# A pooling mixer's output projection: P7 of six blocks as seven smaller products that share P1's and P6's time

## The chip, the cores and the metric

The kernel runs on one core of a Trainium2 chip. The metric is the device time of one execution in microseconds (us). A core has a matrix engine (TensorE, PE in the profile; its weight loads have a row of their own, PEld), three engines for elementwise work (VectorE or DVE, ScalarE or ACT, GpSimd or POOL) and SyncE (SP), which here issues most of the DMAs. Each engine works through its own list of instructions in order; an instruction that waits holds up everything behind it on that engine.

## The reference

One layer of a streaming encoder over x, 4096 rows of 1024 columns, all in float32:

```python
normed = rms_norm(x, norm_w)
u, gate = split(normed @ in_w, 2)               # in_w: 1024 x 2048
pooled = trailing means of u over 2, 4, 8, 16 rows (by column group) - u
mixed = einsum('bsgc,gcd->bsgd', pooled, group_w) + group_b
y = mixed * scale * silu(gate)
out = rms_norm(x + y @ out_w, final_norm_w)     # out_w: 1024 x 1024
```

What this case is about is the last line: the product `y @ out_w`, the addition of x and the closing norm. The kernel calls it the output stage.

## The kernel before, in words

**Seven products.** Each large product is computed as a Winograd form of Strassen's scheme: both operands are cut into quarters, and seven products P1 to P7 of quarter-sized operands (sums and differences of the quarters) take the place of eight. A product's operand is float32, split into a high and a low part (`split`: a copy on ScalarE, L175, then a subtraction on VectorE, L169), and multiplied in three passes, high by high, high by low, low by high (`mm3`, L779). Operand pairs lie in *op* tiles, a ring of four (`next_op`); the weights' pairs of all seven products stay in *w* tiles. Results collect in PSUM, in eight *banks* of 128 x 512. A sum of two products that the scheme wants is made in the bank itself: only P1 and P7 start their bank afresh, the others add to a bank that a copy has filled.

**Stages.** Two input stages, a and b (four blocks of 1024 rows each), make u and the gate, and pool and store y into the DRAM tiles *yd*. The output stage, o, has eight blocks of 512 rows, numbered 0 to 7, in the order P1, P7, P6, P2, P5, P4, P3 (`ORDER_OUT`). A whole product there is 24 matmuls with 512 columns: two row tiles of 128 rows, each with four inner steps of three passes. In `sets_of` a block gets four pairs of banks: x (P1, P2), v (P7, P4), y (P6, P5, P3, on top of a copy of P1's result) and a spare pair; the pairs rotate from block to block.

**What is done twice already.** A quarter-sized product can itself be cut into seven, with 42 matmuls of 256 columns in place of 24 of 512. The kernel before does that at one place of stage b (`product_seven`, L725, with a bank addition at L762), and for P2 of blocks 2 to 7 in the output stage (`product_inner`, L879). P2's five inner products P2, P3, P4, P1, P7 are issued in P2's place, P6 in the middle of P5 and P5 behind it; `add_inner` (L889) adds the latter two's banks to the row tiles on VectorE. `split_inner` makes the operands from one y tile: the plain quarters in one op tile, four sums in another. `load_inner` and `form_inner` make the inner weights in block 1, in four *st* tiles that are kept from then on (`kept`).

**Buffers.** Working tiles of 512 KB come from two first-in, first-out pools, `st` (11) and `vt` (8): `take()` gives the one longest free, `give()` returns one. Which data share a tile, and so who waits for whom, follows from the order of takes and gives in the program's text. A wait is on the last user of the tile: a load into a tile waits for the store that reads it.

**A block's data.** `load_o` takes four y tiles per block (quarters named 11, 21, 22, 12), each 512 KB, on SP's queue (L1045). The main loop runs it four products ahead (`load_reach`), and `split_o` two ahead (`split_reach`): while P1 of a block runs, P6's operand is being split, and so on, across blocks. For P7 `split_o` takes a further tile, subtracts (11 minus 21), and splits. `load_h` takes *row tiles*, two for each half of 256 rows, `hs[b][half, j]`; the result rows are collected in them. Before the last block only half 0 has a DMA there, of x's right half (256 KB each, L1056). x's other quarters are added by POOL's accumulating DMAs (`add_h`, L1062) after the eviction. The last block loads x outright (L1052).

**Eviction.** `evict_o` copies P7's, P6's and P2's banks to the row tiles (ScalarE), copies P1's to the pair y, and adds P5's, P4's and P3's banks to the row tiles (VectorE, L1245). After P4 (half 1) and P3 (half 0) `finish` ends the rows: two squares with their sums on ScalarE (L1121), each into a scratch tile from `take()`, a root (ScalarE L216, the rest on POOL, L217 to L235), two scalings on VectorE (L1125) and two stores on SP's queue (L1129). These run while the next block's P1 and P7 are on TensorE. The last block ends with finer pieces (`early_half` to `late_vector`, L1145 to L1204).

**Order.** A scheduler puts each engine's instructions in order, in the main by the order of the program's text and by dependences; `tc.issue_after(x)` adds the rule that what is inside comes after instruction x. `latest` is the last matmul, `latest_copy` and `latest_split` the last two halves of a split.

## Time and profile before

| | us |
|---|---|
| median of three timed runs | 909.32 |
| their range | 909.14 to 909.33 |
| the profiled execution's own time | 909.13 |
| span of the profiled execution | 907.3 |
| the difference, around the span | 1.8 |

The profile describes one execution. Its page gives each engine's busy time, then the span in 40 slices, the DMA queues, the chain of work that ended last, and the costliest groups of instructions: line, engine, operation, tiles (output <- inputs, without buffer numbers), shapes and count, then busy time, mean ns of one, and idle time before them with what ended it. "L779" is the line in the kernel's text, that of the helper where one is used. Matmuls overlap, so the mean of one is longer than the distance from one to the next. DMA groups give the time from issue to landing.

### The profile page before, as it was taken

The numbers are of one execution on the slowest core, as the hardware profiler recorded it, in microseconds if no ns is written. First come the engines' busy times: TensorE is split into PE (matmuls) and PEld (weight loads), VectorE is DVE, ScalarE is ACT, GpSimd is POOL, SyncE is SP. The second block draws the span as 40 slices with busy tenths as digits, with TensorE's granted clock in tenths as the row PEclk, the third lists the DMA queues.
The fourth block names the chain that finished last, engine by engine and source line by source line (L and its number), as shares of the span: only waits on it lengthen the run. The fifth ranks groups of instructions, "written<-read, shape, count | busy, mean of one in ns | idle before, by whom it ended". The sixth has DMA issues, their size and how long they took to land.

```text
span 907.3 us, 11824 instructions
## 1 busy us (share of the span) xinstructions
PE 898.9 (99%) x4392; PEld 790.2 (87%) x4392; DVE 731.5 (81%) x868; ACT 494.0 (54%) x760; POOL 83.9 (9%) x166
## 2 busy tenths in 40 slices
PE   9999999999999999999999999999999999999996
PEld 7888888888888888889889888888888898988986
DVE  3889896985995999798599499599759768868686
ACT  7869547447446565346545636545535435445434
POOL 0020100100110000000000000001122113112200
PEclk9999999999999999999999999999999999999998
DMA  9987667677575462323554475528585675775732
GB/s 341 401 303 238 251 229 229 215 270 251 224 267 198 161 217 85 110 100 116 206 189 148 176 267 168 192 70 232 173 232 172 171 192 158 169 220 162 175 140 92
DMA packets 71401, 179.41 MB, mean 198 GB/s; under 512 B 6576, under 2 KB 24624, under 8 KB 71344
## 3 DMA queue, kind: packets, MB, share of 16 engines
q1 hardware_dynamic: 58720, 146.13, 46.4%
q0 software_dynamic: 11904, 31.48, 13.5%
q10 hardware_dynamic: 720, 1.06, 0.3%
q8 instruction: 34, 0.56, 0.3%
q14 instruction: 23, 0.19, 0.1%
HBM read 117.81 MB, written 60.83 MB: 197 GB/s over the span
## 4 chain that ended last, share of the span: by engine, by line
PE 95%; DVE 2%; DMA 1%; ACT 1%; issue 0%; DVEq 0%; ACTq 0%
PE bank L779 89%; PE bank L879 3%; PE bank L725 2%; PE bank L421 1%; DMA st<-in_x 1%; DMA early<-in_wut 0%; ACT st L461 0%; DVE vt L1245 0%; ACT st L1152 0%; PE bank L487 0%; DVE vt L172 0%; DVE w L169 0%; ACT st L443 0%; ACT early L443 0%; DVE vt L1204 0%
## 5 line engine op out<-in xcount | busy, mean ns | idle before, releaser
L779 PE MATMUL bank<-op,w 128*128 128x512 f32 x2592 | 560.9, 379 | 0.0
L779 PEld LDWEIGHTS bank<-op,w 128*128 128x128 f32 x2592 | 489.4, 189 | 70.2 <-ACT vt L175 0.4
L779 PE MATMUL bank<-w,op 128*128 128x512 f32 (+1 forms) x1212 | 262.2, 377 | 0.0
L779 PEld LDWEIGHTS bank<-w,op 128*128 128x128 f32 x1212 | 226.0, 189 | 31.0
L169 DVE TENSOR_TENSOR op<-st,op 128x1024 fp32r<-128x1024 f32 x134 | 162.3, 1219 | 58.0 <-ACT op L175 57.6
L175 ACT ACTIVATE op<-st 128x1024 fp32r<-128x1024 f32 x134 | 140.2, 1052 | 113.4 <-PE bank L779 64.5
L175 ACT ACTIVATE vt<-bank 128x512 f32<-128x512 f32 (+1 forms) x115 | 65.8, 590 | 46.5 <-PE bank L779 43.1
L169 DVE TENSOR_TENSOR st<-st,st 128x1024 f32<-128x1024 f32 (+1 forms) x42 | 45.8, 1104 | 18.9 <-ACT st L256 16.8
L169 DVE TENSOR_TENSOR op<-vt,op 128x1024 fp32r<-128x1024 f32 x42 | 51.1, 1219 | 8.1 <-ACT op L175 8.1
L175 ACT ACTIVATE op<-vt 128x1024 fp32r<-128x1024 f32 x42 | 44.1, 1054 | 24.9 <-PE bank L779 20.9
L1062 POOL DMA_DIRECT2D st<-in_x x19 | 16.8, 893 | 387.0 <-DVE op L169 352.9
L175 ACT ACTIVATE st<-bank 128x512 f32<-128x512 f32 (+1 forms) x61 | 34.7, 585 | 30.6 <-PE bank L779 19.1
L175 ACT ACTIVATE bank<-bank 128x512 f32<-128x512 f32 (+1 forms) x60 | 32.1, 537 | 30.1 <-PE bank L779 26.0
L933 DVE TENSOR_TENSOR_SCAN vt<-vt,window 128x1040 f32<-128x1040 f32 x16 | 37.9, 2376 | 1.6 <-DMA yd<-vt 1.5
L169 DVE TENSOR_TENSOR w<-st,w 128x1024 fp32r<-128x1024 f32 (+1 forms) x26 | 30.8, 1198 | 9.2 <-ACT w L175 9.2
L175 ACT ACTIVATE w<-st 128x1024 fp32r<-128x1024 f32 (+1 forms) x26 | 26.6, 1035 | 17.4 <-PE bank L779 9.5
L175 ACT ACTIVATE vt<-tails 128x32 f32<-128x32 f32 x28 | 6.3, 228 | 46.8 <-DVE vt L933 25.7
L979 DVE SCALAR_TENSOR_TENSOR vt<-vt,vt 128x1024 f32<-128x1024 f32 x24 | 29.3, 1219 | 0.3
L172 DVE TENSOR_TENSOR st<-st,vt 128x1024 f32<-128x1024 f32 x22 | 26.1, 1215 | 3.4 <-DMA vt<-rd 3.4
L1125 DVE SCALAR_TENSOR_TENSOR vt<-vt,ors,st 128x1024 f32<-128x1024 f32 x18 | 22.5, 1282 | 7.6 <-POOL ors L235 7.6
L1245 DVE TENSOR_TENSOR st<-bank,st 128x512 f32<-128x512 f32 x23 | 15.8, 689 | 14.0 <-PE bank L779 14.0
L984 DVE SCALAR_TENSOR_TENSOR st<-vt,colt,st 128x512 f32<-128x512 f32 x38 | 26.8, 743 | 0.1
(143 smaller groups left out, 735.3 us busy)
## 6 DMA issues: line engine op xcount, KB each, us to landing
st<-in_xt SPq DMA_DIRECT2D x28, 512.0 KB, 6.3
sd<-st POOLq DMA_DIRECT2D x28, 512.0 KB, 4.0
st<-sd SPq DMA_DIRECT2D x26, 512.0 KB, 4.2
st<-in_x SPq DMA_DIRECT2D x20, 512.0 KB, 6.0
st<-yd SPq DMA_DIRECT2D x20, 512.0 KB, 4.6
yd<-st SPq DMA_DIRECT2D x19, 512.0 KB, 3.1
out<-vt SPq DMA_DIRECT2D x18, 512.0 KB, 4.6
st<-wod SPq DMA_DIRECT2D x15, 512.0 KB, 4.0
```

Source lines behind the costliest of these rows:

```text
L169: return nc.vector.tensor_tensor(out=dst, in0=a, in1=b, op=ALU.subtract)
L172: nc.vector.tensor_tensor(out=dst, in0=a, in1=b, op=ALU.mult)
L175: return nc.scalar.activation(dst, src, func)
L725: latest[0] = nc.tensor.matmul(cell(n, c).rearrange("p (a s) -> p a s", s=2), x1, x2, start=i == P1 and k + m == 0, stop=k == 1 and m == 2 ...
L779: latest[0] = nc.tensor.matmul(ps, a, b, start=start and n == 0, stop=stop and n == 2, skip_group_check=True).ins
L879: latest[0] = nc.tensor.matmul(ps, x1, x2, start=i in (P1, P7) and k + n == 0, stop=k == 1 and n == 2, skip_group_check=True,).ins
L933: nc.vector.tensor_tensor_scan(out=sums_[:, HIST:], data0=flat[:, HIST:], data1=flat[:, HIST - win : 2 * end - win], initial=first_sum, op ...
L979: nc.vector.scalar_tensor_tensor(out=s[:, :, at : at + H], in0=s[:, :, at : at + H], scalar=1.0 / win, in1=v[:, :, HIST:], op0=ALU.mult, o ...
L984: nc.vector.scalar_tensor_tensor(out=sg[:, j], in0=s[:, j, at : at + H], scalar=bias_c[2 * grp + j], in1=sg[:, j], op0=ALU.add, op1=ALU.mult,)
L1062: nc.gpsimd.dma_start(out=hs[b][half, j][:, n], in_=x[row_of(b, half, j), n * H : (n + 1) * H], accum_op=ALU.add,)
L1125: nc.vector.scalar_tensor_tensor(out=us[j], in0=us[j], scalar=rs[:, j : j + 1], in1=fw[0], op0=ALU.mult, op1=ALU.mult,)
L1245: partial["added"] = nc.vector.tensor_tensor(out=dst, in0=src, in1=dst, op=ALU.add).ins
```

## The change

- **P7 of blocks 2 to 7 becomes seven inner products**, which all collect in P7's own pair of banks, v. `split_own` makes the operands: four subtractions of 256 columns into a working tile, then two op tiles, plain quarters and sums, in place of one. `leaf` issues one inner product (6 matmuls of 256 columns) and is shared with P2's.
- **`own_first`**: inner P1 and P5 are issued inside P1, ahead of the last 6 of its 24 matmuls. Two moves on ScalarE follow: cell 1 to cell 0 in the banks (a cell is half a bank), and cell 3 to *m5*, a quarter of the first row tile of half 1, which P6 fills later (in block 7 a tile of its own).
- **`own_rest`**, in P7's place: inner P2 and P6, move of cell 1 to cell 2, `piece(0)` (the first 6 matmuls of P6), inner P7 and P3, move of cell 2 to cell 3, `piece(1)` (6 more of P6), inner P4, and on VectorE an addition of m5 to both halves of bank 1 of the pair. P6 then has 12 matmuls left.
- **Inner weights**: P7's are formed in block 1 as well, ahead of P2's (`forming`): their raw tiles are loaded, summed in place, and split into three kept tiles and a quarter of P7's own w tiles. P2's follow, the last of them in block 2's P1. Six kept st tiles take the place of four.
- **P2's inner products**: their order becomes P2, P4, P1, P3, P7, and their sums are split later (`late_split`, called when the main loop is at P6), the plain quarters where they were.
- **Row tiles**: before the last block, `load_h` runs at P1 (half 1) and P2 (half 0) of the block itself, in `run`, in place of four products ahead in `load_o`.

The diff, without the inner weights' formation and the rewriting of P2's operand tables:

```diff
+    def split_own(u):
+        at = u.rearrange("p (g k) (j c) -> p g j k c", g=2, j=2)
+        b11, b12, b21, b22 = (at[:, g, j] for g in range(2) for j in range(2))
+        v = take("p (n k c) -> p n k c", n=4, k=2)
+        sub(v[:, 0], b12, b11)
+        sub(v[:, 1], b22, v[:, 0])
+        sub(v[:, 2], b22, b12)
+        sub(v[:, 3], b21, v[:, 1])
+        plain_op = next_op("p (s g k j c) -> p s g j k c", s=2, g=2, k=2, j=2)
+        split(plain_op.rearrange("p s g j k c -> p s (g k) (j c)"), u)
+        sums_op = next_op("p (s n k c) -> p s n k c", s=2, n=4, k=2)
+        split(sums_op, v)
...
+    def own_into(i, n, start=False):
+        leaf(own["t"], own_w, i, own["v"][n % 2], n // 2, start)
...
+    def own_move(dst, src):
+        with tc.issue_after(own.get("moved", latest_copy[0])):
+            own["moved"] = copy(own["m5"] if dst is None else own_cell(dst), own_cell(src)).ins
+
+    def own_first(t, b, sets):
...
+        own_into(P1, 1, True)
+        own_into(P5, 3)
+        if b == NBO - 1:
+            own["held"] = take()
+            own["m5"] = own["held"][:, 0, 0:256]
+        else:
+            own["m5"] = hs[b][1, 0][:, 0, 0:256]
+        own_move(0, 1)
+        own_move(None, 3)
+
+    def own_rest(piece):
+        own_into(P2, 0)
+        own_into(P6, 1)
+        own_move(2, 1)
+        piece(0)
+        own_into(P7, 2)
+        own_into(P3, 1)
+        own_move(3, 2)
+        piece(1)
+        own_into(P4, 2)
+        bank = own["v"][1].rearrange("p (j b) -> p j b", j=2)
+        add(bank, bank, own["m5"].unsqueeze(1).to_broadcast([P, 2, 256]))
...
-            for p in (P2, P3, P4, P1, P7):
+            for p in (P2, P4, P1, P3, P7):
                 product_inner(p)
...
         elif i == P2:
             s["12"] = load_y(b, 0, 1)
-            load_h(b, 1)
-        elif i == P5:
+            if b == NBO - 1:
+                load_h(b, 1)
+        elif i == P5 and b == NBO - 1:
             load_h(b, 0)
...
+            if b > 1:
+                t = split_own(s["3"])
+                give(s.pop("3"))
+                return t
...
-        if kind == "o":
+        if kind == "o" and b < NBO - 1 and i in (P1, P2):
+            load_h(b, int(i == P1))
+        if kind == "o" and b > 1 and i == P1:
+            t = split_up.pop(n)
+            out_part(P1, t, sets["x"][0], 0, range(4))
+            out_part(P1, t, sets["x"][1], 1, range(2))
+            own_first(split_up.pop(n + 1), b, sets)
+            with tc.issue_after(latest[0]):
+                out_part(P1, t, sets["x"][1], 1, range(2, 4))
+            evict_o(b, i, sets)
+        elif kind == "o" and b > 1 and i == P7:
+            def piece(m):
+                with tc.issue_after(latest[0]):
+                    out_part(P6, split_up[n + 1], sets["y"][0], 0, range(2 * m, 2 * m + 2))
+            own_rest(piece)
+            evict_o(b, i, sets)
...
+            while b > 0 and len(gathered) < 6 and st.free and len(st.free) + len(vt.free) > 4:
+                gathered.append(st.keep())
+                kept.append(gathered[-1])
...
+        if kind == "o" and i == P6 and late_split:
+            late_split.pop()()
```

More of the change, by code (lines that the diff above doesn't have):

```diff
@@ new lines, with leaf @@
+    own = {}
+    def leaf(t, ws, i, bank, half, start=False):
+        ps = bank.rearrange("p (a s) -> p a s", s=2)[:, half * P : (half + 1) * P]
+        with tc.issue_after(latest[0]):
+            for k in range(2):
+                a = [o[:, k] for o in t[i]]
+                b = [o[:, k].rearrange("p s a -> p a s") for o in ws[i]]
+                for n, (x1, x2) in enumerate(((a[0], b[0]), (a[0], b[1]), (a[1], b[0]))):
+                    latest[0] = nc.tensor.matmul(
+                        ps, x1, x2, start=start and k + n == 0, stop=k == 1 and n == 2,
+                        skip_group_check=True,
+                    ).ins
@@ L867, in product_inner @@
+    def own_rest(piece):
[10 more added lines that the diff above has]
+        add(bank, bank, own["m5"].unsqueeze(1).to_broadcast([P, 2, 256]))
+        if "held" in own:
+            give(own.pop("held"))
     def product_inner(i):
-        t, sets = inner["t"], inner["sets"]
+        sets = inner["sets"]
@@ L892, in sets_bank, with out_part @@
         return inner["sets"]["spare"][n]
+    def out_part(i, t, dst, j, ks, cols=slice(0, H // 2), apart=False):
+        rows = slice(j * P, (j + 1) * P)
+        for k in ks:
+            wk = w[i][k // 2]
+            mm3(
+                dst,
+                (t[:, 0, k, rows], t[:, 1, k, rows]),
+                (wk[:, 0, k % 2], wk[:, 1, k % 2]),
+                (i in (P1, P7) or apart) and k == 0,
+                k == 3,
+                cols,
+            )
     def product_out(i, t, sets, last):
```

159 lines of the change are left out of this document (89 added, 70 removed).

## Prediction

> **What bounds the kernel now.** I read the page first, then TensorE's timeline over the output stage, then busy time block by block. In a timeline row stand the start, the length, the engine, the line, the operation, its tiles and how many were merged, and in brackets the idle time before it and what ended it; in a row of stretches its length, then the busy time of PE, PEld, DVE, ACT and POOL.
>
> ```profile
> PE 898.9 (99%) x4392; PEld 790.2 (87%) x4392; DVE 731.5 (81%) x868; ACT 494.0 (54%) x760; POOL 83.9 (9%) x166
> PEclk9999999999999999999999999999999999999998
> PE 95%; DVE 2%; DMA 1%; ACT 1%; issue 0%; DVEq 0%; ACTq 0%
> ...
> 701.02 1.50 PE L879 MATMUL bank<-w,op 128*128 128x256 f32 x12
> 702.36 0.83 PE L879 MATMUL bank<-inner,op 128*128 128x256 f32 x6
> ...
> 710.89 26.07 PE L779 MATMUL bank<-w,op 128*128 128x512 f32 x120
> 736.79 1.50 PE L879 MATMUL bank<-w,op 128*128 128x256 f32 x12
> ...
> 701.02:736.79 35.77, 35.77 (x188) 31.91 (x186) 26.13 (x34) 17.61 (x27) 7.22 (x16) 1.00 0.80 216
> 736.79:772.56 35.77, 35.77 (x188) 31.91 (x186) 27.35 (x35) 17.53 (x27) 9.78 (x16) 1.00 0.57 138
> ```
>
> TensorE (PE) is busy 99% of the span at full clock and the chain of waits is 95% TensorE; in the output stage each block of 512 rows is 35.77 us of matmuls with no idle in between. So only fewer matmuls shorten it, and any wait that reaches TensorE is added in full. Cadence comes from starts, not from the "mean of one": 710.89 to 736.79 holds 120 matmuls of 512 columns, 0.216 us each; 701.02 to 702.36 holds 12 of 256 columns, 0.112 each. VectorE (DVE) works 26 to 27 us of a block, ScalarE (ACT) 17.6.
>
> **The gain.** P7 in one block is 24 x 0.216 = 5.18 us; as seven products it is 42 x 0.112 = 4.69. That is 0.49 us a block, 2.9 us in six, against a profiled execution of 909.13 us (span 907.3; the three timed runs have a median of 909.32). About 0.2%, 1.8 us, is what a measurement of this kernel can tell from no change. So all added waits together may cost 1.1 us if the change is to show as a gain.
>
> Clock of a changed block, t = 0 at P1's first matmul, nothing waiting, six matmuls of 512 taking 1.30 and one inner product 0.67: P7's inner P1 and P5 end at 4.56 and 5.23, P1 at 6.52, P7's P2 and P6 at 7.19 and 7.86, piece of P6 9.16, P7's P7 and P3 9.83 and 10.50, second piece 11.79, P7's P4 12.46, rest of P6 15.05, P2's first three inner products 17.06, its P3 and P7 18.40, half of P5 20.99, then P2's inner P6.
>
> **Added work.** Durations for it: four groups (busy time and mean ns of one), then ScalarE's timeline, once in the input stage's own seven-product P7 and once at an eviction of P1.
>
> ```profile
> L169 DVE TENSOR_TENSOR op<-st,op 128x1024 fp32r<-128x1024 f32 x134 | 162.3, 1219 | 58.0 <-ACT op L175 57.6
> L175 ACT ACTIVATE op<-st 128x1024 fp32r<-128x1024 f32 x134 | 140.2, 1052 | 113.4 <-PE bank L779 64.5
> L169 DVE TENSOR_TENSOR st<-st,st 128x256 f32<-128x256 f32 x6 | 2.5, 421 | 0.1
> L762 DVE TENSOR_TENSOR bank<-bank,st 128x512 f32<-128x512 f32 x2 | 1.4, 696 | 0.9 <-PE bank L725 0.9
> ...
> 418.07 1.05 ACT L175 ACTIVATE op<-st 128x1024 fp32r<-128x1024 f32 x1
> 419.02 0.38 ACT L175 ACTIVATE bank<-bank 128x256 f32<-128x256 f32 x1
> 419.32 0.38 ACT L175 ACTIVATE st<-bank 128x256 f32<-128x256 f32 x1
> ...
> 726.63 0.58 ACT L175 ACTIVATE bank<-bank 128x512 f32<-128x512 f32 x1 [1.50 <-PE bank L779]
> ```
>
> Per block VectorE gets four subtractions of 256 columns (1.7), one more low-half split (1.2) and the addition of m5 in the bank (0.7), 3.6 us; ScalarE one more high-half copy (1.05) and four moves (0.37 each), 2.5 us. By the totals they fit: 31 of 35 and 20 of 35 us. Block 1 forms two sets of inner weights instead of one (two more DMAs of 512 KB, some 5 us more VectorE work); P7 to P3 there are whole products with steps of 5.18 us, which hides it: 0, at most 1 us. What decides is the order in which each engine meets its waits; I took it from the built program.
>
> **The row tiles.** The two of half 1 now take their places when P1 runs, without a DMA before the last block; the two right halves of x (256 KB each, SP's queue) are issued when P2 runs, between the stores of the previous block's rows on SP's queue, and first read by P3's eviction from t = 27: nothing waits for them, 0 us. What the late taking does change is who shares a tile with whom, which is steps 2 to 4; ScalarE's move to m5 waits for the store of the previous row in that tile, issued at 0.1, with 6.8 as the point from which it costs.
>
> **Step 1, the wait at P7's inner P4, all six blocks.** On ScalarE the copy for the high half of P2's sums stands ahead of the move of cell 2 into cell 3. Both wait for P7's inner P3; P4 may write cell 2 only after the move. From TensorE's end to a ScalarE start is 0.2 us (P1 ends at 721.25 + 24 x 0.216 = 726.43, the copy of its bank starts at 726.63; 721.25 is 710.89 + 48 x 0.216); the copy occupies 0.95 (418.07 to 419.02), the move 0.37: 1.52, plus some 0.05 to TensorE, against the second piece's 1.30. Wait 0.3 us a block, 1.8 in all; bounds 0 and 0.5.
>
> **Step 2, blocks 3, 4 and 5: a load that VectorE waits for.** With six tiles kept instead of four, the reload of the next block's second y tile takes the tile of a row just finished. Its subtraction for the next P7 stands on VectorE directly ahead of the m5 addition, the low half of P2's sums, P5's, an addition, P4's, P3's, and the addition after which P2's inner P6 may reuse its bank. The same chain of reuse in before, in the timelines of VectorE and of SP's queue, with the time from issue to landing of the single DMA (the last number of a DMA row):
>
> ```profile
> 722.39 0.68 DVE L1245 TENSOR_TENSOR vt<-bank,vt 128x512 f32<-128x512 f32 x1
> 726.05 2.48 DVE L1125 SCALAR_TENSOR_TENSOR vt<-vt,ors,st 128x1024 f32<-128x1024 f32 x2 [1.21 <-POOL ors L235]
> ...
> 727.37 1.53 SPq L1129 DMA_DIRECT2D out<-vt  x2
> ...
> out<-vt SPq DMA_DIRECT2D x1, 512.0 KB, 3.6
> ...
> 731.03 0.38 SPq L1045 DMA_DIRECT2D vt<-yd  x1
> ...
> vt<-yd SPq DMA_DIRECT2D x1, 512.0 KB, 5.1
> ...
> 834.44 2.48 DVE L1125 SCALAR_TENSOR_TENSOR vt<-vt,ors,st 128x1024 f32<-128x1024 f32 x2 [1.21 <-POOL ors L235]
> ...
> vt<-yd SPq DMA_DIRECT2D x1, 512.0 KB, 7.7
> ...
> 845.66 1.23 DVE L169 TENSOR_TENSOR st<-st,vt 128x1024 f32<-128x1024 f32 x1 [4.44 <-DMA vt<-yd]
> ...
> 752.55 0.68 DVE L1245 TENSOR_TENSOR vt<-bank,vt 128x512 f32<-128x512 f32 x1
> 753.15 1.22 DVE L166 TENSOR_TENSOR vt<-vt,vt 128x1024 f32<-128x1024 f32 x1
> 754.28 1.22 DVE L169 TENSOR_TENSOR op<-st,op 128x1024 fp32r<-128x1024 f32 x1
> ```
>
> In the block whose P1 starts at 721.25, the row is scaled from t = 4.8, stored at 6.1, its tile reloaded from 9.8, landed 5.1 later: t = 14.9. In the block with P1 at 828.56 (three periods of 35.77 later) VectorE stood still 4.44 us for such a load, and the subtraction began at t = 17.1. There nothing urgent stood behind it. In the changed block VectorE gets there at 10.3 and is held to L, the landing. Behind it, six operations start 1.14 apart (753.15 to 754.28) and one is followed after 0.60 (752.55 to 753.15) before the last, which ends 0.42 after its start: L + 7.9. P2's inner P6 is due at 20.99, so TensorE is late by L - 13.1. (At P2's inner P3 the low half of the sums comes at L + 3.0 against 17.3, the smaller wait.) I take L = 15.5, nearer to the 14.9, whose row starts at the same place: 2.4 us, step 1 included; bounds 0.3 (L below 13.4) and 4.0 (17.1). Three blocks: 7.2.
>
> The Trainium skill ("DMA: Bandwidth & Descriptors", "Anatomy of one DMA") fits a transfer as 2.0 us plus bytes over 436 GB/s, for another issuing path; 512 KB would be 3.2 us. By it L were 6.2 + 3.2 + 3.2 = 12.6 and these blocks would lose only step 1. The rows here, 3.6 out and 5.1 and 7.7 back, disagree.
>
> **Step 3, block 2: P1's leaves.** Here P7's operands come late and ScalarE's queue is full. VectorE's order is: end of P4's eviction, an addition, low half, reciprocal, two of P7's subtractions, two row scalings (1.28 each), a third subtraction, both evictions of P3 (0.68), the fourth between them, a subtraction, then the low half that P7's inner P5 reads. From a reciprocal at t = -1.6 and the 1.2 us that POOL's root takes (726.05's wait), the scalings run -0.4 to 2.1 and that half ends at 6.3; P5 needs it at 4.8: 1.5 late. ScalarE then still has two weight copies (0.5 each), two row squares, a copy of 0.95, a root of 0.3 and two more weight copies ahead of the first move. ScalarE's rows for these, and what a row's store took near P1's start of two blocks:
>
> ```profile
> 723.11 1.06 ACT L1121 ACTIVATE vt<-vt 128x1024 f32<-128x1024 f32 x1 [0.82 <-DVE vt L1245]
> 724.07 0.19 ACT L1121 ACTIVATION_READ_ACCUMULATOR vt<-vt 128x1 f32 x1
> 724.35 0.29 ACT L216 ACTIVATE otmp<-oss,eps 128x2 f32<-128x2 f32 x1
> ...
> 689.59 1.06 ACT L1121 ACTIVATE st<-vt 128x1024 f32<-128x1024 f32 x1 [0.73 <-DMA out<-st]
> ...
> 763.55 1.06 ACT L1121 ACTIVATE st<-vt 128x1024 f32<-128x1024 f32 x1 [1.45 <-DMA out<-st]
> ...
> out<-st SPq DMA_DIRECT2D x1, 512.0 KB, 2.9
> ...
> out<-st SPq DMA_DIRECT2D x1, 512.0 KB, 5.2
> ```
>
> A square occupies 1.2 (723.11 to 724.35). From a start at 3.4: 0.95 + 0.5 + 0.5, squares to 7.8, 8.8, 9.1, 10.1, move done at 10.4. P7's inner P2 was due at 6.52: 3.9 us, the 1.5 included, with step 1 4.2. Bounds 0.3 and 5.5 (the squares write into tiles being stored, which in before held such a square for 0.73 and 1.45).
>
> **Step 4, block 7.** The squares again write into tiles being stored (763.55 was held until t = 6.5, its P1 being at 757.02); the second is followed by the first move. Store issued at 1.5, landed 2.9 to 5.2 later, taken as 5.8, square to 7.0, move to 7.4 against 6.52: 0.9, with step 1 1.2. Bounds 0.3 and 2.5. Block 6 has step 1 alone. After P5 of block 7 the order is as before; the tail costs 0.
>
> **Sum.** 909.13 - 2.9 + 4.2 + 7.2 + 0.3 + 1.2 = 919.1 us.
>
> **Rivals.** (a) *It does what it was built to do*: the waits stay off TensorE. Decided by L below 13.1 and block 2's first move before t = 6.5. 909.13 - 2.9 = 906.2, with up to 1 us of step 1 left, 907.2. For it: totals fit, no output-stage stall in before. Against: the landings above. Faster. 10%. (b) *Step 1 alone*: 909.13 - 2.9 + 1.8 = 908.0, no difference that can be told. 8%. (c) *Loads land in time but P1's queues are late* (also where the skill's fit leads): 909.13 - 2.9 + 4.2 + 0.3 x 4 + 1.2 = 912.8, L below 13.4. 20%. (d) *All at the upper bounds*, loads as slow as the 7.7 us one: 909.13 - 2.9 + 5.5 + 12 + 0.5 + 2.5 = 926.7; 12% for anything above 924. My forecast, 914 to 924, keeps 50%.
>
> "TensorE: Matmul & The Clock Gate" in the Trainium skill ("HAM oscillation") halves TensorE's clock after idle gaps of about 3.4 us. The longest single gap here is 2.4 us, in block 2; no run shows such a gap, and it would lead towards (d).
>
> Range 908 to 925: from (b) to just above 924, leaving out (a) and most of (d). Faster by over 0.2%: 0.10; within: 0.08; slower: 0.82.
>
> **What would show it.** TensorE's timeline in blocks 3 to 5 should show gaps ahead of P2's inner P3 and inner P6, VectorE idle 4 to 6 us on a DMA of a y tile right before the m5 addition. Block 2 should have gaps at P7's inner P5 and P2 whose releasers are VectorE and ScalarE; each block one of 0.3 us at inner P4, released by ScalarE. Matmuls: 188 + 18 a block in the changed ones, at 0.112 and 0.216. If the reloads land before t = 13, or the squares run before t = 3, I am wrong on the slow side; if the built order is not what the trace shows, the whole argument falls.

## The result, and the profile after

| | before | changed |
|---|---|---|
| median, us | 909.33 | 920.5 |
| lowest and highest of four runs, us | 909.14, 910.63 | 918.21, 921.52 |
| the profiled execution, us | 909.13 | 918.21 |
| its span, us | 907.3 | 916.4 |

The ratio is 1.0116, 95% interval 1.0094 to 1.0138: 11 us slower; the forecast was 919.1. The profiled execution is the fastest of the four, so the losses below add up to its 9.1 us of span and not to 11.

The page of the changed kernel, with the rows that answer to those shown of before:

```profile
PE 901.2 (98%) x4500; PEld 792.0 (86%) x4500; DVE 753.5 (82%) x914; ACT 507.2 (55%) x796; POOL 81.2 (9%) x166
...
PE 89%; DMA 3%; DVE 3%; ACT 1%; issue 1%; POOL 0%; SPq 0%; DVEq 0%; POOLq 0%; ACTq 0%
```

TensorE has 108 matmuls more, 18 in each of six blocks as the change says, and it is no longer the whole chain: 89% instead of 95%. To see where, I cut the span at one point of each block, the start of P2's inner P5 (its last), and call these points marks. In a row stand the stretch, its length, the busy time of PE, PEld, DVE, ACT and POOL, the granted clock, and the DMA share and rate. The rows are those of blocks 3 to 7, each from the mark of the block before to its own:

```profile
715.69:753.06 37.37, 36.08 (x206) 31.98 (x205) 31.49 (x45) 19.28 (x32) 7.40 (x16) 1.00 0.68 176
753.06:788.66 35.60, 35.59 (x205) 31.90 (x204) 29.60 (x40) 19.57 (x32) 7.41 (x16) 1.00 0.65 172
788.66:824.95 36.29, 35.81 (x205) 31.90 (x204) 29.60 (x40) 19.58 (x32) 7.38 (x16) 1.00 0.68 181
824.95:860.51 35.56, 35.55 (x205) 31.98 (x204) 26.34 (x34) 19.70 (x31) 7.47 (x16) 1.00 0.70 198
860.51:898.30 37.79, 36.08 (x205) 32.13 (x204) 33.15 (x46) 16.16 (x25) 4.51 (x12) 1.00 0.35 107
```

A changed block without a wait would be 35.77 - 0.49 = 35.28, and the first mark would stand at 710.22 - 0.49 = 709.73 (710.22 is that point in before, 0.67 ahead of the row at 710.89 in the prediction). So block 2 lost 5.96 us (715.69 - 709.73), block 3 2.09, block 4 0.32, block 5 1.01, block 6 0.28, block 7 2.51: 12.2 in all. Less six times 0.49 that is 9.2, and the span grew by 9.1. The busy column hides part of it (35.28 would be all work): short waits lie inside rows that count as busy. The periods don't hide them.

**Block 2** (TensorE's timeline; in brackets the idle time before the row and what ended it):

```profile
690.34 0.49 PE L919 MATMUL bank<-w,op 128*128 128x256 f32 x2 [0.17 <-ACT op L175]
692.06 0.71 PE L919 MATMUL bank<-w,op 128*128 128x256 f32 x4 [1.23 <-DVE op L169]
692.61 1.46 PE L779 MATMUL bank<-w,op 128*128 128x512 f32 x6
695.90 0.94 PE L919 MATMUL bank<-w,op 128*128 128x256 f32 x6 [1.83 <-ACT bank L175]
...
697.64 2.77 PE L779 MATMUL bank<-w,op 128*128 128x512 f32 x6
700.21 1.61 PE L919 MATMUL bank<-inner,op 128*128 128x256 f32 x12
```

By starts, P7's inner P5 lost 0.33 (high half) and 1.50 (low half, VectorE), and its inner P2 lost 1.99 (695.90 against 692.61 + 1.30) to ScalarE's first move. On ScalarE's timeline that move, the last row, stands behind two row squares, a copy and two weight copies:

```profile
691.24 1.04 ACT L1221 ACTIVATE vt<-vt 128x1024 f32<-128x1024 f32 x1
...
693.32 1.04 ACT L175 ACTIVATE op<-st 128x1024 fp32r<-128x1024 f32 x1
...
694.97 0.61 ACT L175 ACTIVATE inner<-vt 128x512 fp32r<-128x512 f32 x1
695.49 0.36 ACT L175 ACTIVATE bank<-bank 128x256 f32<-128x256 f32 x1
```

Then came something else: the first piece of P6, six matmuls of 512, went from 697.64 to 700.21, 2.57 us for what takes 1.30. The stretch's granted clock, the number 0.56 in the row below, says why; with its neighbours it cost 1.8 us.

```profile
696.60:700.20 3.60, 3.60 (x15) 3.06 (x14) 3.00 (x4) 1.76 (x4) 0.39 (x3) 0.56 0.69 244
```

**Block 3** (TensorE, VectorE, ScalarE). VectorE stood 3.49 us for a y tile, which landed at 741.80, 15.1 after P1's start (715.69 + 0.67 + 48 x 0.216 = 726.73), and the addition that P2's inner P6 needs ended 7.8 later:

```profile
744.82 0.71 PE L919 MATMUL bank<-w,op 128*128 128x256 f32 x4 [0.37 <-DVE op L169]
749.69 0.94 PE L919 MATMUL bank<-inner,op 128*128 128x256 f32 x6 [0.90 <-DVE vt L978]
```

```profile
741.80 1.23 DVE L169 TENSOR_TENSOR vt<-st,vt 128x1024 f32<-128x1024 f32 x1 [3.49 <-DMA vt<-yd]
...
749.22 0.42 DVE L978 TENSOR_TENSOR vt<-bank,vt 128x256 f32<-128x256 f32 x1
```

```profile
737.30 1.06 ACT L175 ACTIVATE op<-vt 128x1024 fp32r<-128x1024 f32 x1 [2.10 <-PE bank L919]
738.26 0.37 ACT L175 ACTIVATE bank<-bank 128x256 f32<-128x256 f32 x1
```

The ScalarE pair is the wait at P7's inner P4: the copy first, the move 0.96 later. It is in every changed block.

**Block 7** (TensorE, VectorE, ScalarE): the low half for P7's inner P5 comes late behind two row scalings and two evictions, and inner P4 waits for its move. The first move on ScalarE (last row) ends at 879.59, 0.3 us before TensorE, itself late, asks for it.

```profile
878.07 0.71 PE L919 MATMUL bank<-w,op 128*128 128x256 f32 x4 [1.21 <-DVE op L169]
885.74 0.94 PE L919 MATMUL bank<-w,op 128*128 128x256 f32 x6 [0.39 <-ACT bank L175]
```

```profile
871.39 1.28 DVE L1225 SCALAR_TENSOR_TENSOR vt<-vt,ors,st 128x1024 f32<-128x1024 f32 x1 [0.64 <-POOL ors L235]
...
876.79 1.22 DVE L169 TENSOR_TENSOR op<-vt,op 128x1024 fp32r<-128x1024 f32 x1
```

```profile
875.24 1.07 ACT L175 ACTIVATE op<-vt 128x1024 fp32r<-128x1024 f32 x1 [5.56 <-DVE vt L169]
...
879.23 0.36 ACT L175 ACTIVATE bank<-bank 128x256 f32<-128x256 f32 x1
```

### The profile page after: what moved, and what is told of

The parts are those of the page before. It is cut to its first block, busy times and chain, and to the rows that moved or that the text cites. A ratio compares the mean times of both kernels' runs of the same rounds, so it can differ in the third digit from the quotient of the medians.

```text
span 916.4 us, 12122 instructions
## 1 busy us (share of the span) xinstructions
PE 901.2 (98%) x4500; PEld 792.0 (86%) x4500; DVE 753.5 (82%) x914; ACT 507.2 (55%) x796; POOL 81.2 (9%) x166
## 4 chain that ended last, share of the span: by engine, by line
PE 89%; DMA 3%; DVE 3%; ACT 1%; issue 1%; POOL 0%; SPq 0%; DVEq 0%; POOLq 0%; ACTq 0%
PE bank L779 81%; PE bank L919 5%; PE bank L725 2%; DMA early<-in_wut 2%; DMA st<-in_x 1%; DVE op L169 1%; DMA out<-vt 1%; DVE vt L1345 0%; ACT vt L1221 0%; DVE vt L1225 0%; PE bank L421 0%; ACT vt L1252 0%; DVE vt L166 0%; DVE st L166 0%; DVE vt L172 0%
## 5 line engine op out<-in xcount | busy, mean ns | idle before, releaser
L779 PE MATMUL bank<-w,op 128*128 128x512 f32 (+1 forms) x1068 | 236.4, 378 | 0.0
L779 PEld LDWEIGHTS bank<-w,op 128*128 128x128 f32 x1068 | 197.9, 190 | 26.1
L169 DVE TENSOR_TENSOR op<-st,op 128x1024 fp32r<-128x1024 f32 x124 | 150.3, 1218 | 46.3 <-ACT op L175 45.8
L175 ACT ACTIVATE op<-st 128x1024 fp32r<-128x1024 f32 x124 | 129.9, 1052 | 83.9 <-PE bank L779 43.3
L175 ACT ACTIVATE op<-vt 128x1024 fp32r<-128x1024 f32 x58 | 61.0, 1055 | 53.7 <-PE bank L779 18.6
L169 DVE TENSOR_TENSOR op<-vt,op 128x1024 fp32r<-128x1024 f32 x58 | 70.4, 1219 | 12.6 <-ACT op L175 12.6
L1155 POOL DMA_DIRECT2D vt<-in_x x27 | 26.2, 998 | 441.1 <-DVE vt L1026 352.8
L919 PEld LDWEIGHTS bank<-w,op 128*128 128x128 f32 x288 | 37.1, 191 | 10.4 <-ACT bank L175 5.1
L919 PE MATMUL bank<-w,op 128*128 128x256 f32 x288 | 40.0, 279 | 5.4 <-DVE op L169 2.8
L919 PE MATMUL bank<-inner,op 128*128 128x256 f32 x216 | 29.7, 279 | 1.4 <-DVE vt L978 0.9
L919 PEld LDWEIGHTS bank<-inner,op 128*128 128x128 f32 x216 | 27.7, 194 | 3.0 <-DVE vt L978 1.5
```

Source lines behind the costliest of these rows:

```text
L169: return nc.vector.tensor_tensor(out=dst, in0=a, in1=b, op=ALU.subtract)
L175: return nc.scalar.activation(dst, src, func)
L779: latest[0] = nc.tensor.matmul(ps, a, b, start=start and n == 0, stop=stop and n == 2, skip_group_check=True).ins
L919: latest[0] = nc.tensor.matmul(ps, x1, x2, start=start and k + n == 0, stop=k == 1 and n == 2, skip_group_check=True,).ins
L1155: nc.gpsimd.dma_start(out=hs[b][half, j][:, n], in_=x[row_of(b, half, j), n * H : (n + 1) * H], accum_op=ALU.add,)
```

## The experiments

Theory: the 0.49 us a block is real, and the loss is made of four places where one instruction stands ahead of another in the queue of VectorE or ScalarE; taking such a place away gives its price back. Rival: the six kept tiles leave too few buffers, so that a load, or an engine's backlog, comes late wherever one instruction is moved. Each of the twelve was timed beside the kernel before, whose medians there were 909.17 (e1 to e4), 909.3 (e5 to e8), 909.68 (f0 to f2) and 909.52 (g). Where P7 is whole in a block after block 1 (e3, e4, e6, e8, g), one quarter of one of its weight tiles holds an inner weight, so that part of the output is another product of the same size.

| run | median, us | ratio, 95% interval | first mark | periods of blocks 3 to 7 |
|---|---|---|---|---|
| before | 909.33 | 1 | 710.22 | 35.77 each |
| changed | 920.5 | 1.0116 (1.0094 to 1.0138) | 715.69 | 37.37, 35.60, 36.29, 35.56, 37.79 |
| e1 | 918.72 | 1.0104 (1.0087 to 1.0121) | 717.71 | 35.67, 35.56, 35.56, 35.56, 37.79 |
| e2 | 918.81 | 1.0102 (1.0087 to 1.0117) | 717.35 | 37.97, 35.60, 36.01, 35.28, 37.49 |
| e3 | 920.05 | 1.0117 (1.0102 to 1.0132) | 719.97 | 35.55, 35.56, 36.01, 35.55, 37.80 |
| e4 | 919.6 | 1.0112 (1.0097 to 1.0127) | 719.07 | 36.94, 35.77, 35.77, 35.77, 35.77 |
| e5 | 919.44 | 1.0110 (1.0097 to 1.0123) | 716.00 | 36.57, 36.55, 36.56, 36.56, 37.79 |
| e6 | 909.41 | 1.0002 (0.9993 to 1.0010) | 710.31 | 35.77 each |
| e7 | 918.19 | 1.0098 (1.0083 to 1.0112) | 712.88 | 36.55, 36.56, 36.57, 36.56, 38.12 |
| e8 | 920.85 | 1.0123 (1.0110 to 1.0136) | 712.05 | 38.71, 38.90, 38.65, 37.54, 35.77 |
| f0 | 916.8 | 1.0078 (1.0065 to 1.0091) | 715.74 | 37.42, 35.56, 35.55, 35.56, 37.80 |
| f1 | 916.56 | 1.0077 (1.0064 to 1.0089) | 714.96 | 39.98, 35.28, 35.28, 35.28, 37.56 |
| f2 | 917.05 | 1.0078 (1.0065 to 1.0092) | 716.53 | 39.25, 35.48, 35.28, 35.28, 37.58 |
| g | 908.3 | 0.9987 (0.9978 to 0.9996) | 711.68 | 35.77, 35.28, 35.28, 35.40, 35.88 |

Marks and periods are of one profiled execution each. The first mark also holds what a run lost ahead of block 2, most of it to loads of the input in the first 35 us (0 to 2.4 us). Where a wait stands just ahead of a mark, a clock lowered behind it counts to the period that follows.

### One wait of the chain at a time

**e1, the subtraction out of the way in blocks 3 to 5.** The next block's subtraction goes behind the first addition that P2's inner P6 waits for.

```diff
-            sub(s["3"], s["11"], s["21"])
+            with tc.issue_after(first_added[0]) if b in (4, 5, 6) else nullcontext():
+                sub(s["3"], s["11"], s["21"])
...
-            add_inner(0, (0, 0))
+            first_added[0] = add_inner(0, (0, 0))
```

> The next block's subtraction for P7 (blocks 4 to 6, 11 minus 21) is ordered behind the addition of P2's inner P5 bank, so VectorE no longer waits for the reload of a y tile with six urgent operations behind it. My theory (step 2): the waits at P2's inner P6 in blocks 3, 4 and 5 go; in the profiled execution of the changed kernel these three blocks are 2.09, 0.33 and 1.01 us longer than 35.28, of which 0.28 each is step 1, so 2.6 us go there and somewhat more in the median of its four runs (918.2 to 921.5): 916.8, between 915.5 and 918.3. Rival: the late tile reaches TensorE another way, through the next block's P7: no gain, 920.5.

918.72 us against 916.8 expected. In blocks 3 to 5 only the 0.28 of inner P4 is left (0.39 in block 3), so step 2 is this subtraction. But block 2, where nothing was edited, now shows a wait of 2.54 (TensorE, then VectorE):

```profile
717.71 0.94 PE L919 MATMUL bank<-w,op 128*128 128x256 f32 x6 [2.54 <-DVE vt L978]
```

```profile
714.71 1.22 DVE L169 TENSOR_TENSOR st<-vt,st 128x1024 f32<-128x1024 f32 x1 [4.16 <-DMA st<-yd]
```

The same subtraction for block 3 stands there too, ahead of three of the four additions. In the changed kernel's own trace its tile was issued on SP's queue at 706.33 (first row) and VectorE waited just as well, but 1.21 only (second row), and TensorE was already late enough not to notice:

```profile
706.33 2.86 SPq L1138 DMA_DIRECT2D st<-yd  x2
```

```profile
712.45 1.23 DVE L169 TENSOR_TENSOR st<-vt,st 128x1024 f32<-128x1024 f32 x1 [1.21 <-DMA st<-yd]
```

The load took 6.1 us there and 8.4 in e1. In an execution with a landing like e1's the changed kernel would lose some 2 us more, which is the distance from the profiled 918.21 to the other three, 919.94 to 921.52; that those had it isn't shown, for they left no trace.

**e2, the moves ahead of the copy of P2's sums.**

```diff
-            late_split.pop()()
+            with tc.issue_after(own["moved"]):
+                late_split.pop()()
```

> ScalarE's copy for the high half of P2's sums is ordered behind the move of cell 2 into cell 3. My theory (step 1): the wait ahead of P7's inner P4, 0.28 us in each of five blocks and 0.67 in block 7, goes: 2.1 us, 918.4, between 917 and 920. Rival: the copy, now 0.4 us later, or the eviction of P7 that the scheduler brings forward, makes something else late: 920.5 or more.

918.81 us, as expected. Block 6 is exactly 35.28, a changed block without a wait: the gain and step 1 are both as worked out. Block 7 gains 0.30. Block 2 shows the load wait again, 2.48, and about half the clock behind it (the 1.63 of the row is 0.83 where nothing waits and 0.94 behind a wait at full clock), which cost 1.3 us, in block 3's period:

```profile
717.35 1.63 PE L919 MATMUL bank<-w,op 128*128 128x256 f32 x6 [2.48 <-DVE vt L978]
```

**e3, P7 of block 2 whole again.** Step 3's leaves are gone there.

```diff
-            if b > 1:
+            if b in (3, 4, 5, 6, 7):
...
-        if kind == "o" and b > 1 and i == P1:
+        if kind == "o" and b in (3, 4, 5, 6, 7) and i == P1:
```

> P7 of block 2 is a whole product again; blocks 3 to 7 keep the seven. Both sets of weights are formed as before. My theory (step 3): block 2 was 5.98 us longer than 35.28 in the profiled execution; as a whole product P7 costs 0.49 more but no leaf waits inside P1: 920.5 - 5.98 + 0.49 = 915.0, between 913.5 and 917. Rival: the crowd of operations in block 2 (weight copies, squares, late subtraction) makes a whole P7 late as well: 918 or more.

920.05 us against 915.0 expected: the rival's number, but not its way. A whole P7 isn't late. With nothing to delay P1, TensorE meets the late y tile in full, at P2's inner P6, and the clock lowered behind the wait costs 3.1 us more (first mark 719.97):

```profile
713.64 1.65 PE L919 MATMUL bank<-inner,op 128*128 128x256 f32 x6 [6.29 <-DVE vt L978]
```

**e4, no P7 in pieces at all.** The rest of the change stays: six kept tiles, late row tiles, P2's new order.

```diff
-            if b > 1:
+            if b in ():
...
-        if kind == "o" and b > 1 and i == P1:
+        if kind == "o" and b in () and i == P1:
```

> No P7 as seven at all; what stays of the change is the six kept tiles, both sets of weights, the late row tiles, P2's new order and its late sums. My theory: without leaves and moves nothing urgent stands behind VectorE's wait for a load, so the time is that of before, 909.3, plus at most 1.5: 909.8, between 909.0 and 911. Rival: the late taking of row tiles and the shorter pool cost by themselves: 913 or more.

919.6 us against 909.8: the theory failed. Without one inner product of P7 the kernel is as slow as with all of them. Almost all of it is in block 2; SP's queue, the DMA's time from issue to landing (last number), VectorE and TensorE:

```profile
702.90 0.66 SPq L1138 DMA_DIRECT2D st<-yd  x1
```

```profile
st<-yd SPq DMA_DIRECT2D x1, 512.0 KB, 6.2
```

```profile
709.18 1.23 DVE L169 TENSOR_TENSOR st<-vt,st 128x1024 f32<-128x1024 f32 x1 [5.42 <-issue]
```

```profile
713.07 1.65 PE L919 MATMUL bank<-inner,op 128*128 128x256 f32 x6 [5.28 <-DVE vt L978]
```

The profile names no releaser for VectorE's 5.42 us ("issue"), but 702.90 + 6.2 is 709.1, and the subtraction reads that tile. Of the 8.85 us that the first mark moved, 5.4 are TensorE's wait and 2.7 the clock lowered behind it (the last row's six matmuls and the twelve that follow took 6.00 instead of 3.26).

### All subtractions out of the way

**e5, the subtraction behind all four additions, in every block.**

```diff
-            sub(s["3"], s["11"], s["21"])
+            with tc.issue_after(all_added[0]) if b > 2 else nullcontext():
+                sub(s["3"], s["11"], s["21"])
```

> The next block's subtraction for P7 is ordered behind the last additions of P2's inner products (in P5's place), in blocks 2 to 6. Theory after the first four runs: one y tile, loaded into the tile that P5's split of block 2 frees, lands at 709 to 715 us, and VectorE waits for it in front of additions that TensorE needs; block 2 pays for that alone, whatever P7 is. With the subtraction out of the way what is left is block 2's late leaves (5.96 in the profiled execution of the changed kernel, the lower clock included), 0.28 a block in blocks 3 to 6, 2.5 in block 7, less the gain of 2.94: 909.2 - 2.94 + 5.96 + 1.1 + 2.5 = 915.8, between 914.5 and 917. Rival: the subtraction, now late, holds the next block's P7 inside P1 instead: 918 or more.

919.44 us, the rival's number again. Block 2's load wait is gone, but the first move now comes late in blocks 3 to 6, 1.0 us a block (36.55 - 35.28 - 0.28). P7's operand is in time: inner P1 and P5 don't wait there. On ScalarE the move stands behind two row squares, and the first of these waited for an eviction on VectorE (second fence), which ran ahead of the row scalings in the changed kernel and runs behind them here:

```profile
734.45 0.94 PE L919 MATMUL bank<-w,op 128*128 128x256 f32 x6 [0.74 <-ACT bank L175]
```

```profile
731.25 1.06 ACT L1223 ACTIVATE vt<-vt 128x1024 f32<-128x1024 f32 x1 [3.17 <-DVE vt L1347]
```

**e6, e4 with the bar of e5.** P7 whole everywhere, the subtraction behind all four additions.

> No P7 as seven, with the same order of the subtraction as in the run before this one; of the change only the six kept tiles, both sets of weights, the late row tiles and P2's new order and late sums stay. Theory: the wait for that y tile was all of what the fourth run lost, so the time is that of before: 909.3, between 909.0 and 910.5. Rival: late row tiles or kept tiles cost through another queue, too: 912 or more.

909.41 us, no difference from before, as expected. VectorE runs the same subtraction at 711.85, behind the additions, without a wait (no bracket), and a block is as long as before, all of it busy:

```profile
711.85 1.22 DVE L169 TENSOR_TENSOR st<-vt,st 128x1024 f32<-128x1024 f32 x1
```

```profile
710.00:745.77 35.77, 35.77 (x188) 31.97 (x187) 26.79 (x34) 17.52 (x26) 7.24 (x16) 1.00 0.68 185
```

e4 and e6 differ by the place of one VectorE instruction per block, and by 10.2 us, the 2.7 of lowered clock included.

**e8, e4 with the row tiles taken as early as before.** Only the six kept tiles, the weights formed for them, P2's new order and its late sums are left.

```diff
             s["12"] = load_y(b, 0, 1)
-            if b == NBO - 1:
-                load_h(b, 1)
+            load_h(b, 1)
...
-        if kind == "o" and b < NBO - 1 and i in (P1, P2):
-            load_h(b, int(i == P1))
```

> No P7 as seven, row tiles taken as before the change (four products ahead); six kept tiles and both sets of weights stay. The order of takes changes with it, and in block 2 the built order has no subtraction ahead of the urgent additions. Theory (the late taking of row tiles decides which tile, and so which order, the y tile gets): 909.8, between 909.0 and 911.5. Rival: six kept tiles by themselves leave too few buffers: 914 or more.

920.85 us against 909.8, in the rival's range. TensorE waits ahead of P2's last inner product in blocks 3 and 5 (first fence; 2.94 and 2.88 by starts), by the same chain: y tiles reloaded late, an addition late (VectorE in block 5, second fence). Blocks 4 and 6 have no wait: their 3.13 and 1.77 are the clock lowered behind the other two (granted 0.50 from 750.76 to 755.00). So late row tiles are not the cause: without them such waits come in two blocks instead of one and a short one in e4. That the two tiles kept more make the shortage is likely, but not shown by itself, since e8 keeps P2's new order and late sums as well.

```profile
750.76 1.65 PE L919 MATMUL bank<-w,op 128*128 128x256 f32 x6 [2.77 <-DVE vt L978]
...
828.31 1.36 PE L919 MATMUL bank<-w,op 128*128 128x256 f32 x6 [2.71 <-DVE vt L978]
```

```profile
823.44 1.23 DVE L169 TENSOR_TENSOR vt<-vt,st 128x1024 f32<-128x1024 f32 x1 [2.46 <-DMA st<-yd]
...
826.10 1.23 DVE L166 TENSOR_TENSOR st<-st,vt 128x1024 f32<-128x1024 f32 x1 [1.43 <-DMA vt<-yd]
```

**e7, everything at once in all six blocks.** e5's bar, the moves and the operands of P7 in blocks 2 and 7 ahead of other ready work, the last weight copies one product later.

```diff
-        with tc.issue_after(own.get("moved", latest_copy[0])):
+        with tc.issue_after(own.get("moved", own_copy[0])), tc.high_priority():
...
-                t = split_own(s["3"])
+                with tc.high_priority() if b in (2, 7) else nullcontext():
+                    t = split_own(s["3"])
...
-        (2, P1): lambda: (split_weight(P2, P5, P4), end_weights(P2)),
+        (2, P7): lambda: (split_weight(P2, P5, P4), end_weights(P2)),
```

> All six blocks with P7 as seven; the subtraction ordered as in the first run of this call, the four moves on ScalarE at high priority and no longer behind P6's split, P7's operands of blocks 2 and 7 at high priority, the last weight copies formed one product later. Theory (all that the change lost was order on VectorE and ScalarE): gain 2.94 with up to 3 us of the waits of blocks 2 and 7 left: 907.5, between 906.2 and 909.5. Rival: the operations pushed back (squares, row scalings, weight copies) make something else late: 911 or more.

918.19 us against 907.5, missed. Block 2 comes down to 3.15 us lost (712.88 - 709.73), 0.9 of it ahead of the block; that is the least of all versions with six changed blocks. But e5's 1.0 is still in each of blocks 3 to 6 and block 7 loses 2.84. In blocks 3 to 6 the squares that the first move waited behind still stand ahead of it on ScalarE.

### Removing the backlog in block 2

**f0, the weights formed one product earlier,** so that their copies should be out of block 2 (one still ran there, at 692.57), with e1's bar in blocks 2 to 5.

```diff
-        (1, P7): lambda: load_inner(P7),
-        (1, P6): lambda: (sum_inner(P7), split_weight(P7, P5)),
+        (1, P1): lambda: load_inner(P7),
+        (1, P6): lambda: (sum_inner(P7), split_weight(P7, P5, P6, P7)),
...
-        (2, P1): lambda: (split_weight(P2, P5, P4), end_weights(P2)),
+        (1, P3): lambda: (split_weight(P2, P4), end_weights(P2)),
```

> All six blocks with P7 as seven. The inner weights are formed one product earlier and all within block 1, so that their two raw tiles are free in block 2 and the next block's y tile takes the tile of a stored row; the subtraction for P7 of blocks 3 to 6 is ordered behind the first addition of P2's inner products. Theory: block 2 loses its load wait (2.5 to 2.7 in the runs where the leaves' delay did not cover it) and about 1.5 of the 3.8 us of its leaves, since ScalarE has three weight copies less ahead of the first move; 0.28 a block in blocks 3 to 6 and 2.5 in block 7 stay: 909.2 - 2.94 + 2.5 + 1.1 + 2.5 = 912.4, between 911 and 914.5. Rival: the leaves of block 2 are late for the row scalings and squares, whatever the weights do: 914.5 to 917.

916.8 us against 912.4, in the rival's range. TensorE doesn't wait for block 2's first move any more, but only because P7's inner P5 is later still, for the high half of its operand (692.72): the move itself ended at 696.67, against 695.85 in the changed kernel. Block 3's first move is late as well (735.04; TensorE's timeline):

```profile
692.72 0.49 PE L919 MATMUL bank<-w,op 128*128 128x256 f32 x2 [2.33 <-ACT op L175]
...
735.04 0.94 PE L919 MATMUL bank<-w,op 128*128 128x256 f32 x6 [1.59 <-ACT bank L175]
```

The operand's first subtraction on VectorE had waited for a reloaded y tile once more, at the end of block 1, and VectorE's row scalings and the operand's other subtractions then ran 2.4 us later than in the changed kernel:

```profile
678.07 0.43 DVE L169 TENSOR_TENSOR vt<-st 128x256 f32<-128x256 f32 x1 [3.84 <-DMA st<-yd]
```

**f1, f0 with e2 and with P7's inner P5 later,** behind inner P2 and P6, so that P1 needs inner P1 alone; the moves ahead of other ready work.

```diff
     def own_first(t, b, sets):
...
-        own_into(P5, 3)
...
     def own_rest(piece):
...
         own_into(P6, 1)
+        own_into(P5, 3)
```

> As the run before, and the moves at high priority, ahead of P2's sums and no longer behind P6's split, and P7's inner P5 behind its inner P2 and P6 in place of inside P1. Theory: step 1's 0.28 a block goes, P5 no longer waits for its low half; what stays is a square ahead of the first move and P6's late operand in block 2 (1.7) and 0.7 in block 7: 909.2 - 2.94 + 1.7 + 0.7 = 908.7, between 907.2 and 910. Rival: P7's inner P2 and P6, now first, find their copy of cell 1 not done, and wait as P5 did: 912 or more.

916.56 us against 908.7, missed, though blocks 4, 5 and 6 are 35.28, all three without a wait. What is left is in blocks 2, 3 and 7 (TensorE). f0's wait at the end of block 1 is here as well (3.73 at 678.36) and makes block 2's move late. At the end of block 2 VectorE waits for another reloaded y tile (second fence), and block 3's first move comes late behind that. Behind both of TensorE's waits the clock fell, 1.7 us each; in block 3 it fell about a microsecond after the wait (third row, six matmuls that take 1.30):

```profile
694.83 1.48 PE L920 MATMUL bank<-w,op 128*128 128x256 f32 x6 [2.75 <-ACT bank L175]
734.78 0.94 PE L920 MATMUL bank<-w,op 128*128 128x256 f32 x6 [2.78 <-ACT bank L175]
...
737.70 2.31 PE L779 MATMUL bank<-w,op 128*128 128x512 f32 x6
...
878.87 0.94 PE L920 MATMUL bank<-w,op 128*128 128x256 f32 x6 [1.05 <-ACT bank L175]
```

```profile
718.68 1.23 DVE L166 TENSOR_TENSOR st<-st,st 128x1024 f32<-128x1024 f32 x1 [3.62 <-DMA st<-yd]
```

**f2, f1 with P7's operands of block 2 ahead of other ready work.**

```diff
-                t = split_own(s["3"])
+                with tc.high_priority() if b == 2 else nullcontext():
+                    t = split_own(s["3"])
```

> As the run before, and P7's operands of block 2 at high priority, so that P6's high half comes ahead of the second square. Theory: 1 us less in block 2: 907.8, between 906.5 and 909.3. Rival: the row scalings, now later, delay the next reloads: 909.5 or more.

917.05 us against 907.8, missed: block 2's wait shrinks from 2.75 to 2.30, and the load wait opens again behind it (1.32).

```profile
696.14 0.94 PE L920 MATMUL bank<-w,op 128*128 128x256 f32 x6 [2.30 <-ACT bank L175]
716.53 0.94 PE L920 MATMUL bank<-w,op 128*128 128x256 f32 x6 [1.32 <-DVE vt L979]
```

### Only where nothing is late

**g, P7 in pieces in blocks 4, 5 and 6 alone,** with e6's bar for block 3's subtraction, e1's for those of blocks 4 to 6, and e2.

```diff
-            sub(s["3"], s["11"], s["21"])
-            if b > 1:
+            bar = {3: all_added[0], 4: first_added[0], 5: first_added[0], 6: first_added[0]}.get(b)
+            with tc.issue_after(bar) if bar is not None else nullcontext():
+                sub(s["3"], s["11"], s["21"])
+            if b in (4, 5, 6):
```

> P7 as seven inner products in blocks 4, 5 and 6 alone, whole in blocks 2, 3 and 7 (there one quarter of one of its weight tiles holds an inner weight, so that part of the output is another product; the work is the same). The subtraction for block 3's P7 is held behind the last addition of block 2's P2, as in the kernel without any P7 in pieces; those for blocks 4 to 6 behind the first such addition; the sums of P2 are split after the moves. Theory, that the gain of 0.49 us a block is real and the whole loss is the place of single instructions in VectorE's and ScalarE's queues: blocks 2 and 3 35.77 us, blocks 4, 5 and 6 35.28, block 7 without a wait; 909.3 - 3 x 0.49 = 907.8 us, 907.4 to 908.2. Rival, that each border between a block with P7 whole and one with P7 in pieces opens a wait of its own (the first move behind the row squares, or the reloaded y tile): 1 to 3 us at one or both borders, 909 to 912. A middle result of one border alone: the period of block 4 or of block 7 says which.

908.3 us against 907.8 expected, 1.2 us below before, the only version whose interval lies below 1 (0.9978 to 0.9996, less than the 0.2% that the prediction called the limit); 3 x 0.49 would be 1.5, a ratio of 0.9984, inside it. Blocks 3 (P7 whole) and 4 (in pieces) by the stretches between marks, no idle in either; block 5 is 35.28 as well, and blocks 6 and 7 lose 0.1 each:

```profile
711.68:747.45 35.77, 35.77 (x187) 31.98 (x186) 29.29 (x40) 17.51 (x26) 7.24 (x16) 1.00 0.67 187
747.45:782.73 35.28, 35.28 (x205) 32.13 (x204) 29.04 (x39) 19.43 (x31) 7.45 (x16) 1.00 0.66 179
```

It is not a version to keep as it stands, because P7's weights in the blocks with P7 whole would need the quarter back that an inner weight took, a seventh kept tile. That wasn't tried, and e8 shows what tiles kept away from the loads can cost. Six changed blocks without a wait were not reached; whether an order exists that does it in blocks 2, 3 and 7 stays open.

## Why the prediction was right, step by step

The total was right (919.1 against 920.5), the steps less so. 12.9 us of waits were forecast, and the trace lost 12.2, of which 1.8 are a lowered clock. Step 2 was 3.8 too large; the clock (1.8) and step 4 (1.3 too small) nearly made up for it, and that was luck.

- **The gain, 0.49 us a block:** right. Changed blocks without a wait are 35.28 in e2, f1, f2 and g.
- **Step 1, inner P4 behind the copy, 0.3 a block:** right, 0.28; gone in e2.
- **Step 2, blocks 3 to 5, 2.4 each:** the mechanism is right (e1 takes it away), the size was too large. The failed term is L: 15.1 in block 3, and by the same subtraction in blocks 4 and 5 (starts 777.41 and 813.70, P1 at 764.10 and 799.70) 13.3 and 14.0, not 15.5 three times (VectorE stood 3.49, 3.24 and 3.92 us, not 4 to 6). L - 13.1 gives 2.0, 0.2 (where step 1's 0.28 decides) and 0.9; lost were 2.09, 0.32 and 1.01, 3.4 us instead of 7.2. One value for three landings, taken between rows that stood 2 us apart, was the mistake.
- **Step 3, block 2's leaves and first move, 3.9:** right, 0.33 + 1.50 + 1.99 = 3.82, and by its way: the first move was done 10.4 us after P1's start (695.85 against 685.45), as worked out. Not in the sum: the lowered clock behind them, 1.8. The prediction weighed a single long gap, and three short ones did it.
- **Step 4, block 7, 1.2:** too small, 2.5. TensorE waited for the low half of P7's operand, on VectorE behind two row scalings and two evictions, 1.75 by starts; inner P4 lost 0.67 more. The wait that the step named, for the first move behind the squares, was covered by that: the move ended at 879.59, where inner P2 would have been due at 878.06 (875.42 + 12 x 0.112 + 1.30), and in f1, where inner P5 is out of the way, it shows (1.05 at 878.87). Its reason was another as well: ScalarE had stood 5.56 us for VectorE ahead of the squares, and they didn't wait for a store. I had worked out VectorE's order for block 2 and not for block 7.
- **What no step had:** the y reload that step 2 saw in blocks 3 to 5 comes late in block 2 as well, by up to 6 us (e3, e4). In the changed kernel's trace the 3.8 us of step 3 covered it. So the prediction's sum of separate prices was wrong in kind: the waits overlap, and e3 shows that taking 3.9 us away can give 0 back, since the wait that it uncovers brings a lowered clock with it.
- **The rivals:** (a), the waits off TensorE, and (b), step 1 alone, were not so in any version with six changed blocks, and none reached (d). (c), loads in time and P1's queues late, is what e1's blocks 3 to 7 look like (there the subtraction is out of the way of the load), but not its block 2. e4 and e6 tell what the prediction had counted in blocks 3 to 5 alone: the rest of the change without any P7 in pieces makes a load come late in block 2 too, and that is worth 10.2 us (2.7 of them clock) where one subtraction stands badly, and nothing where it doesn't.

## What to carry to other kernels

Where the bounding engine has no slack, a change of 0.2% is decided by the order in the queues beside it: before adding work, list for every block, the first and the last above all, what each in-order queue holds ahead of the one instruction that the bounding engine waits for, and which of those instructions waits for a load. Fewer free buffers can cost something even where no work is added: a load into a tile freed late lands late, and whatever stands behind its reader pays (e4, e8), or nothing does if nobody urgent stands there (e6). Prices of waits that overlap don't add, so undo them together (e6) and not one by one (e1, e3) to learn what a cause is worth, and put new work only where the trace shows slack (g).

## What the runs showed of the hardware

**The granted clock falls after short gaps, and not always.** Six matmuls of 256 columns right behind a wait take 0.94 at full clock and 1.36 to 1.65 where it has fallen. They took so long behind single gaps of 2.48 (e2), 2.71 and 2.77 (e8), 2.75 (f1), 5.28 (e4) and 6.29 us (e3). Behind 2.78 (f1, at 734.78) and 1.96 (f2, at 735.64) they took 0.94 and 1.05, and the fall came about a microsecond later (granted clock 0.56 from 736.41 to 739.84 in f1, 0.61 from 736.48 to 740.70 in f2). Behind 2.54 (e1) and 2.30 (f2, at 696.14) it didn't come. In the changed kernel the clock fell to 0.56 behind three gaps of 0.2, 1.2 and 1.8 within 6 us; in e1, e2 and e5 the same three left it alone. A fall lasted 3 to 6 us and cost 1.3 (e2) to 3.1 us (e3, e8), 1.8 in the changed kernel, as much as a wait. "TensorE: Matmul & The Clock Gate" in the Trainium skill ("HAM oscillation") puts the limit at idle gaps of about 3.4 us; these rows put falls below that, at 2.0 to 2.8 us.

**A load of 512 KB took 6.1 to 8.4 us from issue to landing at the same place in block 2.** It took 6.1 in the changed kernel (issued at 706.33), 6.2 in e4 (702.90), 7.1 in e2 (707.18) and 8.4 in e1 (706.25). While these ran, POOL's accumulating transfers took 40, 49, 58 and 60% of the DMA engines' time. In before, the prediction's two loads of that size took 5.1 and 7.7 with POOL's transfers at some 20 and 25%, and a store 3.6 with none of them. That they are the reason isn't shown: the 7.7 doesn't fit. The spread of 2 us between executions of nearly the same program is almost as large as the 2.9 us that the change could gain.
